# Channel MLP of a hybrid encoder: the down projection in pairs of hidden blocks with seven block products for eight, and the order of four engines written out

## The chip, the cores and the metric

One core of a Trainium2 chip runs the whole program in one launch. The metric is the device time of that core in microseconds. Engines are named as in the profile: PE is TensorE (matmuls; PEld its weight loads), DVE is VectorE, ACT is ScalarE, POOL is GpSimd, SP is SyncE, which here only issues DMAs.

## The reference

Two layers run over a prompt of 256 tokens and a sample of 1024 tokens with the same weights. Layer 0 mixes tokens with a bidirectional RWKV-7 recurrence, layer 1 with neighbourhood attention. Each layer ends with a squared-ReLU MLP; the change lies in that MLP and what surrounds it.

```python
D_MODEL = 1024; SEQ = 256; DEC_SEQ = 1024; D_FF = 4 * D_MODEL

def _sq_relu_mlp(h, w_up, w_down):
    return jnp.square(jax.nn.relu(h @ w_up)) @ w_down

def _trunk(x, p):
    for layer in range(DEPTH):
        h = _rms_norm(x, p['norm_mix_g'][layer])
        y = ...                                   # RWKV-7 (layer 0) or neighbourhood attention (layer 1)
        x = x + y
        x = x + _sq_relu_mlp(_rms_norm(x, p['norm_mlp_g'][layer]), p['w_up'][layer], p['w_down'][layer])
    return x
```

All data are fp32.

## The kernel before

Tokens of both requests stand side by side as 1280 columns in three segments: 0 is the prompt (256 columns), 1 and 2 are the halves of the sample (512 each). Channels lie on the 128 partitions, so 1024 channels are 8 tiles.

An fp32 product is made of three matmuls on rounded parts. Each operand is split into a high part (a cast to fp32r on ACT) and a low part (the operand minus its high part, on DVE or POOL); `mm3` adds high by high, high by low and low by high into one PSUM bank. `wsplit` (L80 to L91) loads a weight block (512 KB), casts it on ACT and subtracts on the engine it is given.

`channel_layer` (L1275 on) does the mixer's output projection, the residual, the norm and the MLP of one layer:

- the projection with `w_o` or `w_no`, eight output tiles, segments 0 and 1 together and then segment 2; its results are added to `x`, and `add_squares` gathers the sums for the norm;
- `scale(s)`: the normed input of the MLP isn't divided by its root mean square. Instead `x` is multiplied by the mean square `ms`, and the end of the MLP multiplies the sum by the reciprocal (`inverse`), which the homogeneous squared ReLU allows;
- the hidden dimension of 4096 goes in 32 blocks of 128. `up(f, s)` (L1353) makes block f for segment s: 24 matmuls over the 8 input tiles (`dense`), ReLU on ACT, square on POOL, high part on ACT, low part on DVE;
- `down(fs, s)` (L1371) multiplies the hidden blocks fs by their rows of `w_down`, into the 8 output tiles one after the other: three matmuls for each block and tile, then DVE adds the PSUM bank to `x` (L1382).

The loop of blocks runs `up(f, s)` and `down([f - 1], s)` for the three segments in turn. The last two blocks are summed in PSUM (`down([30, 31], s)`). In layer 0 each finished output tile is also scaled, stored, split for the next layer's projections (`split_x`) and squared (`add_squares`), and `token_norms` (N) and the first value blocks of the attention (`v_block`, V) are placed between output tiles.

The framework's planner sets the order of instructions on each engine, from its own estimates, except inside `manual_schedule`, where the engines named keep the order in which the program is written. Before, that holds for TensorE alone, from the last downs on. DMA issues on SP stay with the planner in both kernels. A tile of a pool has a name (tag) and `bufs` buffers in rotation; a writer waits until the last reader of the buffer's former content is done. PSUM has one ring of 7 banks (`ps`) and one bank for norms.

Of the kernel before, what the change touches and what calls it, by code (L numbers as in the profile page):

```python
# [13 lines left out]
P = 128  # L14
# [21 lines left out]

class Pieces:
# [11 lines left out]
class Trunk:  # L49
    def __init__(self, ctx, tc, a):  # L50
# [16 lines left out]
        self.dall = self.cp.tile([P, 8, 2, 20], F32, name="dall")  # L67
        self.bonus = self.cp.tile([P, 20, 8], F32, name="bonus")
# [436 lines left out]
    def v_block(self, act, vw, dst, tp, pp, q, tb, scale=1.0, later=False):  # L505

        nc = self.nc
        ps = pp[0].tile([P, 512], F32, name="vps", tag=pp[1])
# [648 lines left out]
    def add_squares(self, wk, x, m, s, acc, nsq=2):  # L1157

        nc = self.nc
        c0, c1 = SEGS[s]  # L1160
        n = c1 - c0
        if m == 0:
            nc.scalar.activation(acc[:, :n], x[s][:, m], AF.Square)
        else:
            sq = wk.tile([P, 512], F32, name="sq", tag="sq", bufs=nsq)
            nc.scalar.activation(sq[:, :n], x[s][:, m], AF.Square)
            nc.gpsimd.tensor_tensor(out=acc[:, :n], in0=acc[:, :n], in1=sq[:, :n], op=ALU.add)
# [9 lines left out]
    def token_norms(self, wk, wh_, pn, acc, s):  # L1177
# [8 lines left out]
        for j in range(2):  # L1186
            for b in range(nb):
                if j and b % 2 == 0:

                    w = 4 // nb  # L1190
                    pq = wh_.tile([P, 256], F32, name="pq", tag="hhFalse", bufs=2)
# [12 lines left out]
    def gate_begin(self):  # L1204
# [36 lines left out]
        def weight(m):  # L1241
            self.wo.append(self.wsplit(self.clw, self.a["w_o"][m], 1024, nc.gpsimd, tag="u"))
# [11 lines left out]
    def gated(self, wk, pm, src):  # L1254

        nc, act = self.nc, self.act
        with self.gctx, self.tc.tile_pool(name="go", bufs=1, reuse_waits="tile", side="right") as gp:
            (sh, sl, ss), (gh, gl, gs) = self.gate
            todo = [(0, k) for k in range(KT)] + [(s, k) for s in (1, 2) for k in range(KT - 1)] + [(1, KT - 1), (2, KT - 1)]
            for s, k in todo:  # L1260
# [5 lines left out]
                ps = pm.tile([P, 512], F32, name="ps", tag="ps")  # L1266
# [7 lines left out]
    def channel_layer(self, layer, x_src, src, wname, dst, gnext=None, gate=False):  # L1274
# [6 lines left out]
        with ExitStack() as ctx:  # L1281
# [7 lines left out]
            pn = ctx.enter_context(tc.tile_pool(name="cln", bufs=1, space=PSUM, reuse_waits="tile"))  # L1289
            wo = self.wo  # L1290
            if gate:
                self.gated(wk, pm, src)
# [13 lines left out]
            def dense(hi, lo, s):  # L1306
                c0, c1 = SEGS[s]
                n = c1 - c0
                ps = pm.tile([P, 512], F32, name="ps", tag="ps")
# [7 lines left out]
            for seg in ((0, 1), (2,)):  # L1317
                for m in range(8):
                    hi, lo = wo.pop(0)
                    if len(wo) < 1 and todo:  # L1320
                        wo.append(self.wsplit(wp, a[wname][todo.pop(0)], 1024, nc.vector, tag="u"))
# [9 lines left out]
                    for s in seg:  # L1331
# [3 lines left out]
                        self.add_squares(wk, x, m, s, ms[s], 2 + layer)  # L1335
# [17 lines left out]
            def up(f, s):  # L1353
                c0, c1 = SEGS[s]
                n = c1 - c0
                if s == 0:
                    wu[f] = self.wsplit(wp, a["w_up"][layer, f], 1024, nc.gpsimd, tag="u")
                ps = dense(*wu[f], s)
                r = wk.tile([P, 512], F32, name="rl", tag="nt", bufs=3 + layer)
                nc.scalar.activation(r[:, :n], ps[:, :n], AF.Relu)  # L1360
                nc.gpsimd.tensor_tensor(out=r[:, :n], in0=r[:, :n], in1=r[:, :n], op=ALU.mult)  # L1361
                hh, hl = (wh_.tile([P, c1 - c0], F32R, name=t, tag=f"{t}{s > 0}", bufs=4 if s else 2) for t in ("hh", "hl"))
                nc.scalar.copy(hh[:, :n], r[:, :n])  # L1363
                nc.vector.tensor_tensor(out=hl[:, :n], in0=r[:, :n], in1=hh[:, :n].bitcast(F32), op=ALU.subtract)  # L1364
                hid[f, s] = hh, hl

            def wdown(f):
                wd[f] = self.wsplit(wd_, a["w_down"][layer, f], 1024, nc.gpsimd, tag="d", rb=1)

            def down(fs, s, between={}):  # L1370
                c0, c1 = SEGS[s]  # L1371
                n = c1 - c0
                parts = [(wd[f], hid.pop((f, s))) for f in fs]
                last = NF - 1 in fs
                if last and gnext is not None:
                    accs[s] = wk.tile([P, 512], F32, name="acc", tag="acc", bufs=2) if s < 2 else wh_.tile([P, 512], F32, name="acc", tag="hhTrue", bufs=4)
                for m in range(8):
                    ps = pm.tile([P, 512], F32, name="ps", tag="ps")
                    for i, ((hi, lo), (hh, hl)) in enumerate(parts):
                        self.mm3(ps[:, :n], hi[:, m * P:(m + 1) * P], lo[:, m * P:(m + 1) * P], hh[:, :n], hl[:, :n], i == 0, i == len(parts) - 1)  # L1380
# [11 lines left out]
            wu, wd, hid, accs = {}, {}, {}, {}  # L1392
            rest = [(s, j) for s, (c0, c1) in enumerate(SEGS) for j in range((c1 - c0) // P)]
            up(0, 0)
            scale(0)
            wdown(0)
            up(1, 0)
# [3 lines left out]
            up(0, 2)  # L1401
            down([0], 0)
# [3 lines left out]
            down([0], 2)  # L1406
            wdown(1)
            for f in range(2, NF - 1):
                for s in range(3):
                    up(f, s)  # L1410
                    down([f - 1], s)
                if rest and f > 4:
                    inverse(*rest.pop())
                wdown(f)
            up(NF - 1, 0)
            up(NF - 1, 1)
            wdown(NF - 1)
            norms = lambda s: self.token_norms(wk, wh_, pn, accs[s], s)
            vw = []

            def block(tb):
                self.v_block(act, vw, self.scr["v1_d"], (wk, "nt", 512, 3), (pm, "ps"), 0, tb, self.tn[:, 0, tb:tb + 1])
            N = lambda s: lambda: norms(s)
            V = lambda tb: lambda: block(tb)
            with tc.manual_schedule(engines={mybir.EngineType.PE}):
                down([NF - 2, NF - 1], 0)
                up(NF - 1, 2)
# [493 lines left out]
```

## Time and profile before

| | |
|---|---|
| time, median of 3 runs | 4051.72 us (4046.44 to 4057.34) |
| span of the profiled execution (first to last instruction) | 4029.3 us; its own device time is not among the three, which lie 17 to 28 us above the span |
| PE busy | 3805.9 us, 94% of the span |
| DVE, ACT, POOL busy | 2244.2, 1580.9, 1338.7 us |
| MLP loop of layer 0, of layer 1 | from about 1545 to 2354 us, from about 3180 to 3992 us of the span |

How to read the lines below: a row of a time view gives start, duration, engine, source line, operation, output and input with their shapes, and in brackets how long the engine stood idle before it and for whom. A row of the windows view gives the stretch, its length, the busy times of PE, PEld, DVE, ACT and POOL (with counts), the granted clock of TensorE as a share of full speed, the DMA share and GB/s. Rows of groups give count, total and mean duration. Matmuls overlap in the records: their distance from start to start is the rate.

### The profile page before, as it was taken

How to read it: one execution, taken by the hardware profiler on the slowest of the kernel's cores; microseconds unless marked ns; L12 is line 12 of the kernel's file. 1: busy time of each engine (PE TensorE's matmuls, PEld its weight loads, DVE VectorE, ACT ScalarE, POOL GpSimd, SP SyncE). 2: the span in 40 equal slices, each digit the busy share in tenths (PEclk: the TensorE clock that was granted, in tenths of full speed). 3: DMA queues.
4: the chain of work that ended last, by engine and by line, in shares of the span. 5: the costliest groups of instructions: out<-in, count | busy, mean ns of one | idle time of the engine just before them, and what ended most of it. 6: DMA issues, size and time to landing. Idle time of an engine off the chain costs nothing.

```text
span 4029.3 us, 90997 instructions
## 1 busy us (share of the span) xinstructions
PE 3805.9 (94%) x36820; PEld 3210.5 (80%) x36820; DVE 2244.2 (56%) x4581; ACT 1580.9 (39%) x3868; POOL 1338.7 (33%) x1252
## 2 busy tenths in 40 slices
PE   8988898888888899999999999999989999999999
PEld 5764578778888788888888889887778888888888
DVE  5778743656564456555555561455554755555555
ACT  6776642555555431111111142565654111111111
POOL 4446542122222433222222250344443422222222
PEclk9987989999999999999999999999999999999999
DMA  4236565766664421101111015354463010110101
GB/s 140 72 104 221 207 222 137 171 171 160 161 153 118 146 79 37 42 32 42 37 37 43 32 71 165 103 124 98 101 199 129 35 42 35 39 42 32 42 32 63
DMA packets 450885, 394.89 MB, mean 98 GB/s; under 512 B 267456, under 2 KB 352832, under 8 KB 450464
## 3 DMA queue, kind: packets, MB, share of 16 engines
q1 hardware_dynamic: 416048, 327.72, 28.7%
q10 hardware_dynamic: 34416, 61.35, 4.1%
q8 instruction: 289, 4.73, 0.5%
q14 instruction: 132, 1.08, 0.1%
HBM read 270.50 MB, written 124.44 MB: 98 GB/s over the span
## 4 chain that ended last, share of the span: by engine, by line
PE 79%; DVE 6%; ACT 5%; DMA 4%; issue 4%; POOL 2%; SPq 1%; ACTq 0%; DVEq 0%; POOLq 0%
PE ps L95 19%; PE ps L96 19%; PE ps L97 19%; PE wu L997 4%; PE vps L512 1%; PE vps L513 1%; PE vps L514 1%; PE aps L997 1%; PE op L1836 1%; PE kps L997 1%; PE lps L997 1%; PE pt L1779 1%; PE ltw L598 1%; PE yps L997 1%; PE yo L997 1%
## 5 line engine op out<-in xcount | busy, mean ns | idle before, releaser
L1382 DVE TENSOR_TENSOR x<-ps,x 128x256 f32<-128x256 f32 x1488 | 814.5, 597 | 643.8 <-PE ps L97 643.7
L95 PE MATMUL ps<-ah,whi 128*128 128x512 f32 (+1 forms) x2304 | 843.2, 366 | 0.0
L96 PE MATMUL ps<-al,whi 128*128 128x512 f32 (+1 forms) x2304 | 825.5, 358 | 0.0
L97 PE MATMUL ps<-ah,wlo 128*128 128x512 f32 (+1 forms) x2304 | 822.6, 357 | 1.5 <-DVE wlo L90 1.3
L90 POOL TENSOR_TENSOR wlo<-raw,whi 128x1024 fp32r<-128x1024 f32 (+1 forms) x178 | 390.2, 2192 | 856.0 <-ACT whi L89 823.8
L95 PE MATMUL ps<-hh,whi 128*128 128x512 f32 (+1 forms) x1536 | 546.5, 356 | 9.8 <-DVE x L1382 9.8
L96 PE MATMUL ps<-hl,whi 128*128 128x512 f32 (+1 forms) x1536 | 545.6, 355 | 0.0
L97 PE MATMUL ps<-hh,wlo 128*128 128x512 f32 (+1 forms) x1536 | 545.1, 355 | 0.0
L95 PEld LDWEIGHTS ps<-ah,whi 128*128 128x128 f32 x2304 | 434.3, 188 | 72.4 <-issue 8.2
L97 PEld LDWEIGHTS ps<-ah,wlo 128*128 128x128 f32 x2304 | 433.4, 188 | 72.6 <-DVE wlo L90 1.7
L96 PEld LDWEIGHTS ps<-al,whi 128*128 128x128 f32 x2304 | 434.4, 189 | 62.3 <-issue 1.0
L89 ACT CAST whi<-raw 128x1024 fp32r<-128x1024 f32 (+1 forms) x206 | 200.4, 973 | 706.3 <-PE ps L96 627.7
L1361 POOL TENSOR_TENSOR rl<-rl 128x512 f32<-128x512 f32 (+1 forms) x192 | 173.8, 905 | 506.1 <-PE ps L97 462.4
L95 PEld LDWEIGHTS ps<-hh,whi 128*128 128x128 f32 x1536 | 290.7, 189 | 54.2 <-DVE x L1382 12.0
L97 PEld LDWEIGHTS ps<-hh,wlo 128*128 128x128 f32 x1536 | 291.0, 189 | 41.6
L96 PEld LDWEIGHTS ps<-hl,whi 128*128 128x128 f32 x1536 | 290.6, 189 | 40.5
L1360 ACT ACTIVATE rl<-ps 128x512 f32<-128x512 f32 (+1 forms) x192 | 100.7, 524 | 555.9 <-PE ps L97 555.9
L1363 ACT CAST hh<-rl 128x512 fp32r<-128x512 f32 (+1 forms) x192 | 105.6, 550 | 324.2 <-POOL rl L1361 324.2
L1364 DVE TENSOR_TENSOR hl<-rl,hh 128x512 fp32r<-128x512 f32 (+1 forms) x192 | 119.8, 624 | 143.1 <-ACT hh L1363 142.5
L1773 POOL TENSOR_TENSOR s<-s,mx 128x384 f32<-128x384 f32 (+1 forms) x150 | 109.7, 744 | 163.2 <-DVE mx L1772 114.2
L872 DVE TENSOR_TENSOR tmp<-mt,q 128x31 f32<-128x31 f32 (+15 forms) x310 | 117.2, 378 | 38.9 <-ACT mt L861 21.0
L1078 POOL TENSOR_TENSOR y<-y,mu 128x512 f32<-128x512 f32 x18 | 19.3, 1074 | 351.2 <-DVE mu L1075 351.2
(304 smaller groups left out, 8265.1 us busy)
## 6 DMA issues: line engine op xcount, KB each, us to landing
raw<-in_w_down_dram SPq DMA_DIRECT2D x64, 512.0 KB
raw<-in_w_up_dram SPq DMA_DIRECT2D x64, 512.0 KB
ar<-ar_d SPq DMA_DIRECT2D x80, 256.0 KB
bk<-bk_d SPq DMA_DIRECT2D x80, 256.0 KB
ar_d<-ar ACTq DMA_DIRECT2D x32, 512.0 KB
bk_d<-bk ACTq DMA_DIRECT2D x32, 512.0 KB
bs<-tab SPq DMA_DIRECT2D x128, 96.0 KB
v_d<-vt ACTq DMA_DIRECT2D x80, 128.0 KB
```

What stands on the lines that cost most here:

```text
L89: nc.scalar.copy(hi[:, cs], raw)
L90: lo_eng.tensor_tensor(out=lo[:, cs], in0=raw, in1=hi[:, cs].bitcast(F32), op=ALU.subtract)
L95: mm(ps, sh, mh, start=first, stop=False)
L96: mm(ps, sh, ml, start=False, stop=False)
L97: mm(ps, sl, mh, start=False, stop=last)
L872: nc.vector.tensor_tensor(out=tv, in0=mt[:, 0:jj, jj:jj + 1].to_broadcast([P, jj, w]), in1=q[:, jj:jj + 1, jj:].to_broadcast([P, jj, w]), ...
L997: self.nc.tensor.matmul(out, w, x, start=start, stop=stop, skip_group_check=free)
L1361: nc.gpsimd.tensor_tensor(out=r[:, :n], in0=r[:, :n], in1=r[:, :n], op=ALU.mult)
L1363: nc.scalar.copy(hh[:, :n], r[:, :n])
L1364: nc.vector.tensor_tensor(out=hl[:, :n], in0=r[:, :n], in1=hh[:, :n].bitcast(F32), op=ALU.subtract)
L1382: nc.vector.tensor_tensor(out=xv, in0=ps[:, :n], in1=xv, op=ALU.add)
L1773: nc.gpsimd.tensor_tensor(out=s[:, :nk], in0=s[:, :nk], in1=mx[:, 2:3].to_broadcast([P, nk]), op=ALU.mult)
```

## The change

For the sample (segments 1 and 2) two hidden blocks and two halves of the output channels form a 2 x 2 by 2 x 2 block product: weights A(i, j) of 128 rows x 512 output channels, with i the half of the output and j the block of the pair, times hidden parts b(j, t), with t the segment. It is done with seven products of sums instead of eight plain ones, in the form with shared partial sums: `pair_steps` defines for each step n a `prep(n)` (the weight sum on POOL and its split into W[n]; the hidden sum on DVE and its split into B[n]), a `product(n)` (4 output tiles, three matmuls of 512 columns each; where the shared sum goes on, the matmuls add to the bank that DVE has just read) and a `prompt(n)`, which uses four of the split weights for the prompt's plain products, two output tiles in one bank. `block_pair` writes out the order: the next pair's ups between the products of the current one. There are 14 such pairs (blocks 2 to 29) in each layer; blocks 0, 1, 30 and 31 go as before.

From block 2's up to the end of `channel_layer`, TensorE, DVE, ACT and POOL all keep the written order. Further: `w_down` is loaded in halves of 256 KB with six raw buffers; the other weights of the layer have one raw buffer where they had two; the seven PSUM banks become rings of 3 (`ps`) and 4 (`pc`); `inverse` is called once per pair; the constants `dall` and `bonus` live in a pool that closes before the first `channel_layer`.

```diff
+MANUAL = {mybir.EngineType.PE, mybir.EngineType.DVE, mybir.EngineType.Activation, mybir.EngineType.Pool}
...
+            def bank(name=None):
+                turn[0] += 1
+                name = name or ("ps", "pc")[turn[0] % 2]
+                return pm.tile([P, 512], F32, name="ps", tag=name, bufs={"ps": 3, "pc": 4}[name])
...
+            def wup(f):
+                wu[f] = self.wsplit(wp, a["w_up"][layer, f], 1024, nc.gpsimd, tag="u", rb=1)
+
+            def split(src, s, pool, tags, bufs, eng):
+                n = src.shape[1]
+                hi, lo = (pool.tile([P, n], F32R, name=t, tag=t, bufs=bufs) for t in tags)
+                nc.scalar.copy(hi, src)
+                eng.tensor_tensor(out=lo, in0=src, in1=hi.bitcast(F32), op=ALU.subtract)
+                return hi, lo
...
+            def up(f, s, name=None, whole=True):
...
+                ps = dense(*wu[f], s, name)
+                r = wk.tile([P, n], F32, name="rl", tag="nt", bufs=6) if s else wh_.tile([P, n], F32, name="rl", tag="np", bufs=2)
+                nc.scalar.activation(r, ps[:, :n], AF.Relu)
+                nc.gpsimd.tensor_tensor(out=r, in0=r, in1=r, op=ALU.mult)
+                hid[f, s] = r
+                if whole or s == 0:
+                    cut(f, s)
+
+            def wraw(f, i):
+                r = raws[f, i] = wd_.tile([P, 512], F32, name="raw", tag="dr", bufs=6)
+                nc.sync.dma_start(r, a["w_down"][layer, f, :, 512 * i:512 * i + 512])
+
+            def wcut(src):
+                return split(src, 0, wd_, ("dh", "dl"), 4, nc.gpsimd)
...
+            def pair_steps(f0, f1):
+                W, B, S, ch = {}, {}, {}, {}
+                A = lambda i, j: raws[(f0, f1)[j], i]
+                b = lambda j, t: hid[(f0, f1)[j], t]
+                tt = lambda eng, o, x_, y_, op: eng.tensor_tensor(out=o, in0=x_, in1=y_, op=op)
+                bcut = lambda src: split(src, 1, wh_, ("hhTrue", "hlTrue"), 3, nc.vector)
...
+                def prep(n):
+                    if n == 0:
+                        W[0], B[0] = wcut(A(0, 1)), bcut(b(1, 1))
+                    elif n == 1:
+                        S["s"] = stile()
+                        tt(nc.gpsimd, S["s"], A(1, 0), A(1, 1), add)
+                        S["t"] = ttile()
+                        tt(nc.vector, S["t"], b(0, 2), b(0, 1), sub)
+                        W[1], B[1] = wcut(S["s"]), bcut(S["t"])
+                    elif n == 2:
+                        tt(nc.gpsimd, S["s"], S["s"], A(0, 0), sub)
+                        s4 = stile()
+                        tt(nc.gpsimd, s4, A(0, 1), S["s"], sub)
+                        W[2], B[2] = wcut(s4), bcut(b(1, 2))
+                    elif n == 3:
+                        W[3], B[3] = wcut(A(0, 0)), bcut(b(0, 1))
...
+                    elif n == 5:
+                        s3 = stile()
+                        tt(nc.gpsimd, s3, A(0, 0), A(1, 0), sub)
+                        t3 = ttile()
+                        tt(nc.vector, t3, b(1, 2), b(0, 2), sub)
+                        W[5], B[5] = wcut(s3), bcut(t3)
...
+                    elif n == 7:
+                        W[7] = wcut(A(1, 0))
+
+                def product(n):
+                    new, seg, row = ((1, 1, 0), (1, 2, 4), (0, 2, 0), (1, 1, 0), (0, 2, 0), (0, 2, 4), (0, 1, 4))[n]
+                    (hi, lo), (hh, hl) = W[n], B[n]
+                    for j in range(4):
+                        if new:
+                            ch[j] = bank("pc")
+                        cs = slice(j * P, j * P + P)
+                        mm = nc.tensor.matmul
+                        mm(ch[j], hi[:, cs], hh, start=bool(new), stop=False, skip_group_check=True)
+                        mm(ch[j], hi[:, cs], hl, start=False, stop=False, skip_group_check=True)
+                        mm(ch[j], lo[:, cs], hh, start=False, stop=True, skip_group_check=True)
+                        xv = x[seg][:, row + j]
+                        nc.vector.tensor_tensor(out=xv, in0=ch[j], in1=xv, op=ALU.add)
...
+            def block_pair(f2, cur, ahead):
+                (prep, product, prompt), f3, final = cur, f2 + 1, ahead is None
+                U = lambda f, s: up(f, s, "ps", False)
+                prep(1)
+                product(0)
+                prompt(0)
+                U(f2, 1)
+                wraw(f3, 0)
+                prep(2)
+                product(1)
+                U(f2, 2)
+                wraw(f2, 1)
+                prep(3)
+                product(2)
+                U(f2, 0)
+                if not final:
+                    wup(f2 + 2)
+                prep(4)
+                product(3)
+                prompt(3)
+                U(f3, 1)
+                wraw(f3, 1)
+                prep(5)
+                product(4)
+                if not final:
+                    U(f3, 2)
+                prep(6)
+                product(5)
+                prep(7)
+                U(f3, 0)
+                wraw(f2, 0)
+                if not final:
+                    wup(f3 + 2)
+                product(6)
+                prompt(6)
+                if not final:
+                    ahead[0](0)
+                prompt(7)
...
-            for f in range(2, NF - 1):
-                for s in range(3):
-                    up(f, s)
-                    down([f - 1], s)
-                if rest and f > 4:
-                    inverse(*rest.pop())
-                wdown(f)
...
+            with tc.manual_schedule(engines=MANUAL):
...
+                for f in range(2, NF - 2, 2):
+                    ahead = pair_steps(f + 2, f + 3) if f < NF - 4 else None
+                    block_pair(f + 2, cur, ahead)
+                    cur = ahead
+                    if rest and f > 4:
+                        inverse(*rest.pop())
...
+                up(NF - 1, 2, None, False)
+                cut(NF - 1, 2, True)
                 down([NF - 2, NF - 1], 0)
-                up(NF - 1, 2)
...
+                    v0 = [self.wsplit(wp, ..., 1024, nc.gpsimd, tag="u", rb=1) for j in range(2)]
```

136 lines of the change are left out of this document (90 added, 46 removed).

## The prediction

> **What bounds the kernel now.** I read the page's chain first, then the busy time by stretches of both MLP loops, then the instructions in order of time of one pass of the loop and of the end of layer 0's MLP.
>
> ```profile
> span 4029.3 us, 90997 instructions
> PE 79%; DVE 6%; ACT 5%; DMA 4%; issue 4%; POOL 2%; SPq 1%; ACTq 0%; DVEq 0%; POOLq 0%
> ```
> ```profile
> 2200.00:2300.00 100.00, 100.00 (x529) 85.81 (x528) 53.03 (x99) 19.69 (x30) 28.82 (x19) 1.00 0.12 43
> 3530.91:3558.83 27.92, 27.92 (x145) 23.76 (x144) 14.71 (x27) 5.23 (x9) 7.46 (x5) 1.00 0.11 38
> 2375.00:2396.00 21.00, 15.87 (x94) 13.07 (x92) 20.52 (x29) 8.87 (x17) 14.18 (x9) 0.99 0.25 94
> ```
> The chain is 79% TensorE. In the two loops TensorE is busy in every microsecond at full granted clock (PEclk, the column behind the five busy times), and one pass over a hidden block takes 27.92 us in which DVE works 14.71, ACT 5.23 and POOL 7.46 us. Only removed matmuls shorten a pass. The third row is the end of layer 0's MLP: there DVE is busy 20.52 of 21 us and TensorE waits.
>
> **The change, part by part**
>
> *Matmuls removed.* First matmuls of the four groups of one pass (start, duration):
> ```profile
> 3508.51 0.28 PE L95 MATMUL ps<-ah,whi 128*128 128x256 f32 x1
> 3511.38 0.28 PE L95 MATMUL ps<-hh,whi 128*128 128x256 f32 x1
> 3514.25 0.39 PE L95 MATMUL ps<-ah,whi 128*128 128x512 f32 x1
> 3519.85 0.40 PE L95 MATMUL ps<-hh,whi 128*128 128x512 f32 x1
> 3525.34 0.39 PE L95 MATMUL ps<-ah,whi 128*128 128x512 f32 x1
> ```
> From start to start: up on the prompt 2.87, down on the prompt 2.87, up on one half of the sample 5.60, down on it 5.49 us. A pair of blocks had eight half-products of 5.49 / 2 = 2.745 us each on the sample; now it has seven. 14 pairs in 2 layers: 28 x 2.745 = **-76.9 us**, if TensorE stays full. A pair then lasts 2 x 27.92 - 2.745 = 53.1 us.
>
> *Work added beside it.* Means by shape:
> ```profile
> L1382 DVE TENSOR_TENSOR x<-ps,x 128x512 f32<-128x512 f32 x992 | 637.3, 686 | 601.2 <-PE ps L97 601.1
> L90 POOL TENSOR_TENSOR wlo<-raw,whi 128x1024 fp32r<-128x1024 f32 x142 | 343.8, 2421 | 763.7 <-ACT whi L89 763.7
> L90 POOL TENSOR_TENSOR wlo<-raw,whi 128x512 fp32r<-128x512 f32 x36 | 46.4, 1288 | 92.3 <-ACT whi L89 60.1 <-DMA vraw<-in_w_nv_dram 24.5 <-PE ps L97 3.8
> L1361 POOL TENSOR_TENSOR rl<-rl 128x512 f32<-128x512 f32 x128 | 133.2, 1041 | 504.6 <-PE ps L97 462.4 <-ACT rl L1360 42.1
> L1364 DVE TENSOR_TENSOR hl<-rl,hh 128x512 fp32r<-128x512 f32 x128 | 90.8, 709 | 115.2 <-ACT hh L1363 114.8
> L1363 ACT CAST hh<-rl 128x512 fp32r<-128x512 f32 x128 | 79.6, 622 | 269.3 <-POOL rl L1361 269.3
> L1360 ACT ACTIVATE rl<-ps 128x512 f32<-128x512 f32 x128 | 76.1, 595 | 434.5 <-PE ps L97 434.5
> L89 ACT CAST whi<-raw 128x1024 fp32r<-128x1024 f32 x170 | 178.2, 1048 | 637.4 <-PE ps L96 622.5 <-issue 5.9 <-DMA raw<-in_w_down_dram 5.7
> ```
> Per pair POOL gets eight half-weight subtractions (8 x 1.29), two whole ones (2 x 2.42), the squares (4 x 1.04 + 2 x 0.6) and four weight sums (priced like a subtraction, 4 x 1.29): 26 us against 14.9. DVE gets 36 evictions of 512 columns (28 for products, 8 for the prompt's two-chunk banks, where there were 32 plus 16 short ones), seven low parts (7 x 0.71), four sums, two short low parts and about one reciprocal: 34 us against 29.4. ACT: about 15 against 10.4. All lie below 53, so no engine takes over as an average. The half-size weight loads double 64 DMA issues on SP, whose queue is idle in between; the bytes stay. The cost is then in the order, since DVE, ACT and POOL now run strictly as written.
>
> *The hand-over between pairs.* I walked through one pair with these durations. Nearly all operands are ready over 1 us ahead, because a block of up (5.6 us) lies behind each preparation. The exception is step 0 of the next pair, written between the last two prompt groups. How a short up passes through the engines:
> ```profile
> 3511.58 0.39 ACT L1360 ACTIVATE rl<-ps 128x256 f32<-128x256 f32 x1 [2.06 <-PE ps L97]
> 3512.04 0.61 POOL L1361 TENSOR_TENSOR rl<-rl 128x256 f32<-128x256 f32 x1
> 3512.68 0.41 ACT L1363 CAST hh<-rl 128x256 fp32r<-128x256 f32 x1 [0.72 <-POOL rl L1361]
> 3513.12 0.43 DVE L1364 TENSOR_TENSOR hl<-rl,hh 128x256 fp32r<-128x256 f32 x1 [0.40 <-ACT hh L1363]
> 3969.78 3.67 DVE L1382 TENSOR_TENSOR x<-ps,x 128x512 f32<-128x512 f32 x6
> ```
> With X the end of the last short up (3511.38 here), its low part is done at X+2.17. ACT then casts the new up weight (to X+2.7), POOL subtracts it (X+2.74 to X+5.14) and only then the weight of step 0 (to X+6.40). DVE meanwhile evicts four product chunks and two prompt banks back to back (0.61 apart, last row) and reaches the low part of step 0 at X+5.7. Whether it can run there:
> ```profile
> 2384.10 1.41 POOL L1167 TENSOR_TENSOR acc<-acc,sq 128x512 f32<-128x512 f32 x1 [0.27 <-ACT sq L1166]
> 2384.30 0.68 DVE L1382 TENSOR_TENSOR x<-ps,x 128x512 f32<-128x512 f32 x1
> 2384.91 1.16 DVE L1175 SCALAR_TENSOR_TENSOR al<-x,vec,ah 128x512 fp32r<-128x512 f32 x1
> 2372.98 1.29 POOL L1384 TENSOR_TENSOR x<-x,ms 128x512 f32<-128x512 f32 x1
> 2373.71 1.11 DVE L1364 TENSOR_TENSOR hl<-rl,hh 128x512 fp32r<-128x512 f32 x1 [4.21 <-ACT hh L1363]
> ```
> An eviction (one input in PSUM) ran its normal 0.68 beside a POOL subtraction or sum, but operations with two SBUF inputs ended 0.56 and 0.55 us after POOL's (2385.51 to 2386.07; 2374.27 to 2374.82). So the low part ends at X+6.40+0.55 = X+6.95. TensorE wants it for the second matmul of product 0: product 6 (2.745) and two prompt groups (1.435 each) and one matmul, X+5.85. Stall 1.15 us. Without the exclusion DVE would end at X+6.4, a stall of 0.6; were that operand early, the low part of the weight (X+6.40, wanted by the third matmul at X+6.1) would be late next, by 0.3. 13 hand-overs x 2 layers x 1.15 = **+30 us** (16 without the exclusion; at the low end 0, if DVE reaches the operand earlier than walked).
>
> The Trainium skill, "SBUF — State Buffer", section "Who interferes with whom", says that a VectorE instruction with two SBUF inputs and a GpSimd instruction that reads SBUF exclude each other for the whole instruction. The trace agrees with its 0.55 us behind POOL's end. By that rule the hand-overs cost the 30 us just taken and the sum below is 4042; with free sharing they would cost 16, and it would be 4028.
>
> *The last pair* of a layer has no up between products 4 and 5, and product 5 adds onto banks that DVE must first read. The low part of step 5 stands ahead of these evictions on DVE and comes some 5.5 us after the start of product 4 (relu 0.6, square 1.04, weight sum 1.29, cast 0.62, subtraction 1.29, 0.55 of exclusion); the first eviction ends at 6.2 where TensorE asks at 2.745. **+3.5 per layer, +7**.
>
> *The end of layer 0's MLP*, so far ordered by hand on TensorE alone, is now in written order on all four. Rows of before:
> ```profile
> 2355.17 0.42 DVE L1382 TENSOR_TENSOR x<-ps,x 128x256 f32<-128x256 f32 x1 [4.34 <-PE ps L97]
> 2367.49 0.68 DVE L1382 TENSOR_TENSOR x<-ps,x 128x512 f32<-128x512 f32 x1
> 2412.81 4.14 DVE L1175 SCALAR_TENSOR_TENSOR al<-x,vec,ah 128x512 fp32r<-128x512 f32 x3
> 2437.66 0.48 ACT L518 ACTIVATE vt<-vps,tn 128x256 f32<-128x256 f32 x1 [1.52 <-PE vps L514]
> 2374.74 0.74 DVE L1175 SCALAR_TENSOR_TENSOR al<-x,vec,ah 128x512 fp32r<-128x512 f32 x1
> 2378.47 0.72 ACT L1174 ACTIVATE ah<-x,vec 128x512 fp32r<-128x512 f32 x1 [2.52 <-DVE x L1384]
> ```
> The first row is the first eviction; the prompt's splits last 12.3 us, the sample's 49.5 (2367.49 to 2416.95), the value blocks end 20.7 later: 82.5 us, with the last up hidden inside. Written order makes each output chunk a loop through engines: eviction 0.6, scaling, ACT's high part 0.75, DVE's low part 0.77, and only then the next eviction; POOL's sum of squares of the chunk before (1.3) holds the port. A chunk scaled on DVE takes 0.6 + wait to 1.3 + 0.55 + 0.75 + 0.77 = 3.4; one scaled on POOL 1.3 + 1.3 + 0.75 + 0.77 = 4.1; eight chunks 28.7 (the first POOL one lacks the sum: 3.5). Two halves: 57.4, and two chains of norms between them (an estimate of 2 each, some ten steps of 0.15 to 0.4): 62. The prompt at 0.42/0.69 of that: 17. The second value weight has one raw buffer now, so its load follows the first one's subtraction, and ACT waits in front of the sample's first chunk:
> ```profile
> 3506.55 0.33 SPq L88 DMA_DIRECT2D raw<-in_w_up_dram  x1
> 3507.50:3509.50 2.00, 2.00 (x15) 1.79 (x14) 1.29 (x3) 1.65 (x2) 0.02 (x1) 1.00 0.78 258
> ```
> A 512 KB load takes about 3 us from issue to the end of its traffic; with cast and subtraction it delays the chain by 7.5. The last hidden block's cut (up, square, cast, subtraction) stands ahead of the first eviction, +2.6, and its up (5.6) now precedes the chain. 5.6 + 2.6 + 17 + 7.5 + 62 + 20.7 = 115.4 against 82.5: **+33 us** (+15 if the chunks overlap better, +45 with a cold clock). Layer 1's end has no such loop: nothing.
>
> *The start of the MLP.* Ten reciprocals per layer ran there (the last two rows are layer 1's):
> ```profile
> L90 DVE TENSOR_TENSOR wlo<-raw,whi 128x1024 fp32r<-128x1024 f32 x28 | 34.6, 1235 | 5.0 <-ACT whi L89 5.0
> 3149.90 2.58 DVE L1351 RECIPROCAL ms<-ms 128x128 f32<-128x128 f32 x3
> 3152.80 0.39 PE L95 MATMUL ps<-hh,whi 128*128 128x256 f32 x1 [3.15 <-DVE x L1382]
> ```
> Three of them stand just ahead of the evictions for which TensorE waits 3.15 us. They move into the pairs, where DVE has 19 us of slack: -3 per layer. Single raw buffers for the projection and up weights make a chain of load 3.05, cast 1.05 and subtraction 1.24 per output chunk, beside 5.6 us of matmuls: it just fits; I put +1.5 per layer for the second up weight. Together **-3** (-6 to +6). The moved constants and the two PSUM rings (7 banks as before) I put at nothing: their last readers end before the first writers here.
>
> Sum: -76.9 + 30 + 7 + 33 - 3 = -10, on the profiled span of 4029.3: 4019. The median of the runs is 22.4 above that span; what lies around the span I leave as it is: 4051.7 - 10 = **4042 us**. The bounds: pairs 0 to 84 (below), end 15 to 45, start -6 to +6.
>
> **The rivals**
>
> *Faster: the pairs run full.* If DVE reaches step 0 without the backlog I walked, the 30 us go: 4012. For it: DVE has 19 us of slack per pair. Against it: the whole weight's subtraction (2.42) stands ahead of step 0 on POOL.
>
> *Faster: the end of layer 0 overlaps as before.* With +10 instead of +33: 4019. For it: before, DVE was full there too (20.52 of 21), so part of my loop may replace waits that already exist. Against it: written order leaves DVE idle during ACT's part of each chunk.
>
> *Slower: up weights land late.* If SP issues the second up weight in written order, it goes behind the last half weight of the next pair, whose buffer frees with POOL's subtraction for step 7, at about X-0.6 (the last sample up ends at X-5.6; relu 0.6, square 1.04, two subtractions of 1.29, one exclusion of 0.55). 768 KB at the rate of the row above (258 GB/s) end near X+3.7, ACT casts there instead of X+1.6, and step 0 slips by 2.1: the stall becomes 3.25, 26 x 3.25 = 84 instead of 30: 4096. It decides once the weight lands after X+2.45 (0.85 us x 26 = 22 more brings it to 4064). Against it: in the trace SP issues the up weight as soon as its buffer is free (3506.55, half a pass ahead of need).
>
> **How the numbers follow.** About 0.3%, 12 us, is what a measurement of this kernel can tell from no change. My forecast has 0.45, with its own range of 4022 to 4062 (0.14 faster, 0.27 same, 0.04 slower); full pairs 0.25 (faster); a better end 0.13 (faster, 0.03 of it same); late weights 0.15 (slower); the rest 0.02. Faster 0.49, same 0.32, slower 0.19. The range of 8 in 10 runs from 4005 to 4082: below it lie full pairs together with a better end, above it the full price of late weights.
>
> **What would show it.** The matmuls of the two loops drop by 336. Between pairs TensorE waits about 1.1 us for a DVE low part, 26 times, at a period near 54.3 us; without these waits full pairs are right, with 3 us late weights. Behind product 4 of the last pair stands one wait of 3 to 4 us for evictions. From the first eviction of layer 0's last down to its last value block there are 105 to 115 us, with DVE waiting for ACT's high parts. The waits of 3.2 us at the MLP's start shrink below 1. Wrong would be the whole picture if POOL or DVE were busy nine tenths of a pair.

## The result and the profile after

The changed kernel takes 4076.97 us in the median of 4 runs (4066.76 to 4086.64), the kernel before 4049.09 (4 runs): ratio 1.0066, 95% interval 1.0045 to 1.0087. It is slower, by 18 to 35 us; 10 us less were forecast. A second series further down gave 1.0070 [1.0055, 1.0085].

The page of the profile after: span, chain, and the groups in which TensorE waits (behind the bar busy time, mean of one, and the idle time ahead with what ended most of it).

```profile
span 4084.8 us, 89789 instructions
PE 69%; DVE 10%; DMA 7%; ACT 6%; issue 4%; POOL 3%; SPq 1%; ACTq 0%; POOLq 0%; DVEq 0%
L96 PE MATMUL ps<-ah,whi 128*128 128x512 f32 (+1 forms) x2304 | 846.1, 367 | 7.9 <-ACT whi L90 7.1
L98 PE MATMUL ps<-ah,wlo 128*128 128x512 f32 (+1 forms) x2304 | 828.3, 360 | 6.2 <-POOL wlo L91 5.3
L1477 PE MATMUL ps<-hlTrue,dh 128*128 128x512 f32 x784 | 311.5, 397 | 15.1 <-DVE hlTrue L1368 15.1
L1476 PE MATMUL ps<-hhTrue,dh 128*128 128x512 f32 x784 | 308.5, 394 | 7.2 <-DVE x L1480 7.2
```
TensorE's share of the chain fell from 79% to 69%, DVE's rose from 6% to 10%. Two of the waits are new in kind: the first two groups, up and projection, had none on a weight worth telling before and now stand 7.1 us for casts on ACT and 5.3 us for low parts on POOL. In e4 below, with two half buffers, they are 2.4 us and none; in e9, the kernel before with single buffers alone, 3.2 and 6.5.

The stages, cut at TensorE's first matmul of each; an MLP start runs from its first norm matmul to the last matmul of block 1's downs, a loop from there to the last downs or the last up ahead of them, so that this up counts to the end in both (us; in brackets an unedited second run of the changed kernel, a0 below):

| stage | before | after | difference |
|---|---|---|---|
| up to layer 0's projection | 1377.5 | 1405.5 (1393.7) | +28.0 (+16.2) |
| of it, end of the scan: last zk cut to last root | 21.0 | 28.1 (26.5) | +7.1 (+5.5) |
| layer 0's projection | 115.3 | 114.4 (113.9) | -0.9 (-1.4) |
| MLP start, layer 0 | 74.4 | 82.4 (79.7) | +8.0 (+5.3) |
| loop, layer 0 | 787.3 | 777.3 (776.2) | -10.0 (-11.1) |
| end of layer 0's MLP | 91.8 | 124.9 (124.9) | +33.1 (+33.1) |
| attention | 562.0 | 567.9 (564.9) | +5.9 (+2.9) |
| layer 1's projection | 117.4 | 120.0 (118.8) | +2.6 (+1.4) |
| MLP start, layer 1 | 75.5 | 82.6 (81.2) | +7.1 (+5.7) |
| loop and end, layer 1 | 828.1 | 809.7 (811.3) | -18.4 (-16.8) |

The spans differ by 55.5, twice what the medians do: the profiled execution of before was faster than all its timed runs, that of after was the slowest of its four. Most of the 28 us ahead of the projection seems of that kind (the same kernel reached it at 1405.5 and at 1393.7); about 6 of them belong to the change (below).

The steady pair, the last pair's products 4 and 5, and the first wait of layer 0's end, from the windows of after:

```profile
1670.63:1725.09 54.46, 53.72 (x279) 45.35 (x277) 33.25 (x50) 14.06 (x25) 27.37 (x21) 1.00 0.13 39
2358.62:2361.38 2.76, 2.76 (x13) 2.06 (x11) 0.00 (x0) 0.60 (x1) 1.83 (x2) 1.00 0.00 0
2361.38:2365.10 3.72, 0.15 (x1) 0.02 (x1) 2.08 (x3) 1.66 (x3) 2.99 (x3) 0.89 0.21 70
2365.10:2370.37 5.27, 5.26 (x13) 4.11 (x14) 4.59 (x8) 1.14 (x2) 1.67 (x2) 0.50 0.01 3
2406.50:2437.60 31.10, 0.57 (x6) 0.44 (x4) 13.70 (x17) 9.93 (x16) 14.91 (x11) 0.59 0.21 76
```
A pair takes 54.46 us with DVE busy 33.3, POOL 27.4 and ACT 14.1 (forecast 54.3, 34, 26 and 15): none of the three is near full. Product 4 of the last pair runs its 2.76 us, then TensorE stands 3.72; the fourth row is taken up in the last section. At the end of layer 0 TensorE works 0.57 us out of 31.1.

The hand-over between two pairs, rows of after in order of time:

```profile
1664.60 0.40 PE L1476 MATMUL ps<-hhTrue,dh 128*128 128x512 f32 x1
1666.35 0.42 DVE L1368 TENSOR_TENSOR hlFalse<-rl,hhFalse 128x256 fp32r<-128x256 f32 x1 [2.44 <-ACT hhFalse L1367]
1667.34 2.41 POOL L91 TENSOR_TENSOR wlo<-raw,whi 128x1024 fp32r<-128x1024 f32 x1 [1.47 <-ACT whi L90]
1669.70 1.30 POOL L1368 TENSOR_TENSOR dl<-raw,dh 128x512 fp32r<-128x512 f32 x1
1670.28 1.27 DVE L1368 TENSOR_TENSOR hlTrue<-rl,hhTrue 128x512 fp32r<-128x512 f32 x1
1670.63 0.39 PE L1476 MATMUL ps<-hhTrue,dh 128*128 128x512 f32 x1
1671.60 0.50 PE L1477 MATMUL ps<-hlTrue,dh 128*128 128x512 f32 x1 [0.58 <-DVE hlTrue L1368]
```
Product 6 starts here at X = 1664.60. The short up's low part ends at X+2.17, the up weight's subtraction at X+5.15, step 0's weight at X+6.40, and DVE's low part of step 0, begun beside it, at X+6.95, 0.55 behind POOL's end: within 0.01 us, the figures of the walk in the prediction. Only TensorE came otherwise. The last two prompt groups took 3.29 us where 2.87 were walked, because they waited for a PSUM bank that DVE had not yet read, so product 0 (last two rows) starts at X+6.03 and not at X+5.62. Its second matmul starts at X+7.00, 1.15 us behind the X+5.85 of the walk.

### The profile page after: what moved, and what is told of

It is laid out like the page before. It is cut to its first block, busy times and chain, and to the rows that moved or that the text cites. A ratio compares the mean times of both kernels' runs of the same rounds, so it can differ in the third digit from the quotient of the medians.

```text
span 4084.8 us, 89789 instructions
## 1 busy us (share of the span) xinstructions
PE 3778.3 (92%) x36484; PEld 3171.2 (78%) x36484; DVE 2337.9 (57%) x4441; ACT 1686.3 (41%) x4128; POOL 1688.6 (41%) x1540
## 4 chain that ended last, share of the span: by engine, by line
PE 69%; DVE 10%; DMA 7%; ACT 6%; issue 4%; POOL 3%; SPq 1%; ACTq 0%; POOLq 0%; DVEq 0%
PE ps L96 12%; PE ps L98 12%; PE ps L97 12%; PE ps L1477 4%; PE wu L998 4%; PE ps L1476 4%; PE ps L1478 4%; DVE x L1480 2%; PE vps L513 1%; PE vps L514 1%; PE vps L515 1%; PE aps L998 1%; PE kps L998 1%; PE op L2001 1%; PE lps L998 1%
## 5 line engine op out<-in xcount | busy, mean ns | idle before, releaser
L1480 DVE TENSOR_TENSOR x<-ps,x 128x512 f32<-128x512 f32 x784 | 484.9, 678 | 0.1
L91 POOL TENSOR_TENSOR wlo<-raw,whi 128x1024 fp32r<-128x1024 f32 (+1 forms) x114 | 235.2, 2064 | 223.0 <-ACT whi L90 211.6
L1477 PE MATMUL ps<-hlTrue,dh 128*128 128x512 f32 x784 | 311.5, 397 | 15.1 <-DVE hlTrue L1368 15.1
L1476 PE MATMUL ps<-hhTrue,dh 128*128 128x512 f32 x784 | 308.5, 394 | 7.2 <-DVE x L1480 7.2
L1478 PE MATMUL ps<-hhTrue,dl 128*128 128x512 f32 x784 | 308.1, 393 | 0.5 <-POOL dl L1368 0.5
L1368 DVE TENSOR_TENSOR hlTrue<-ts,hhTrue 128x512 fp32r<-128x512 f32 x112 | 139.3, 1244 | 217.7 <-ACT hhTrue L1367 217.7
L90 ACT CAST whi<-raw 128x1024 fp32r<-128x1024 f32 (+1 forms) x142 | 133.1, 937 | 189.2 <-PE ps L97 71.4
L1368 POOL TENSOR_TENSOR dl<-raw,dh 128x512 fp32r<-128x512 f32 x128 | 196.5, 1546 | 12.4 <-ACT dh L1367 11.0
L1368 POOL TENSOR_TENSOR dl<-ds,dh 128x512 fp32r<-128x512 f32 x112 | 169.0, 1509 | 63.4 <-ACT dh L1367 63.4
L1477 PEld LDWEIGHTS ps<-hlTrue,dh 128*128 128x128 f32 x784 | 147.8, 188 | 52.1 <-DVE hlTrue L1368 23.4
L1476 PEld LDWEIGHTS ps<-hhTrue,dh 128*128 128x128 f32 x784 | 147.9, 189 | 38.6 <-issue 8.0
```

Of the source, the lines that this page charges most:

```text
L90: nc.scalar.copy(hi[:, cs], raw)
L91: lo_eng.tensor_tensor(out=lo[:, cs], in0=raw, in1=hi[:, cs].bitcast(F32), op=ALU.subtract)
L1368: eng.tensor_tensor(out=lo, in0=src, in1=hi.bitcast(F32), op=ALU.subtract)
L1476: mm(ch[j], hi[:, cs], hh, start=bool(new), stop=False, skip_group_check=True)
L1477: mm(ch[j], hi[:, cs], hl, start=False, stop=False, skip_group_check=True)
L1478: mm(ch[j], lo[:, cs], hh, start=False, stop=True, skip_group_check=True)
```

## The experiments

Times are compared by their ratio to the kernel before, timed beside each; the changed kernel itself has 1.0066 to 1.0070, so 0.001 is 4 us.

**The end of layer 0: written order on TensorE alone (e1_tail).**
```diff
                 cut(NF - 1, 2, True)
+            with tc.manual_schedule(engines={mybir.EngineType.PE}):
                 down([NF - 2, NF - 1], 0)
```


> Only layer 0's (and layer 1's) end is edited: from the last two downs on, only TensorE keeps the written order, as in the kernel before. Theory W (the written order of DVE, ACT and POOL makes the first norms wait behind later evictions): the stretch from the last up group of layer 0 (31, second half of the sample) to the end of its last V block falls from 116 us to 83 to 86, the 31 us wait of TensorE ahead of the first norms' transposes falls below 3, and the time falls by 30 to 33 us, to 4044 to 4047. Rival R1 (the buffers of the new layout set the end: rings shared by relu outputs, squares and V tiles, single raw buffer of the V weights): the stretch stays above 110 us and the time within 5 us of 4077. In both, all other stages stay.

Ratio 1.0011 [0.9993, 1.0030]. The stretch from the end of the last up to the attention's first matmul went from 119.6 to 90.9 us, -28.7: theory W. Counted as in the expectation, from the start of the last up to the last V block, it went from 116.3 to 87.3, a little above 83 to 86; by the ratios the time fell by 22 to 24 us where 30 to 33 were expected. What ACT did in that stretch of after:

```profile
2405.00 1.04 ACT L90 CAST whi<-raw 128x1024 fp32r<-128x1024 f32 x1
2412.58 1.04 ACT L90 CAST whi<-raw 128x1024 fp32r<-128x1024 f32 x1 [6.54 <-DMA raw<-in_w_nv_dram]
2418.57 0.72 ACT L1175 ACTIVATE ah<-x,vec 128x512 fp32r<-128x512 f32 x1 [3.80 <-POOL x L1418]
2436.05 0.72 ACT L1175 ACTIVATE ah<-x,vec 128x512 fp32r<-128x512 f32 x1 [1.99 <-DVE x L1418]
2437.20 0.39 ACT L1193 COPY pq<-acc 128x256 f32<-128x256 f32 x1
PE nps L1196 <- ACT pq L1193: 36.8, 2, 30.6
```
TensorE waits 30.6 us for a copy of 0.39 us (`pq`, last two rows). The prompt's norms are written behind output tile 6 of the next down, so the copy stands in ACT's order behind the second value weight's cast (6.54 us for its load) and six passes of one cast each (2418.57 to 2436.05, two passes per 7.1 us), each waiting for the next scaled tile. In e1 TensorE's waits in this stretch add up to 13 us: 6.4 for evictions and 5.7 for the sums that the norms need are the largest.

**The rest of the end (e8_cover).** The kernel of e1 with the last up behind the first of the last downs again:
```diff
-                up(NF - 1, 2, None, False)
-                cut(NF - 1, 2, True)
...
                 down([NF - 2, NF - 1], 0)
+                up(NF - 1, 2, None, False)
+                cut(NF - 1, 2, True)
```


> The kernel with only TensorE in written order at the end of a layer, with the last up group again between the first and the second of the last downs, as in the kernel before. Theory C (the end of layer 0 is as long as DVE's evictions, cuts and norms; the last up group covers 5.6 us of them only when it lies behind the first down): from the end of the products to the attention 95 us in place of 99.7, some 4.6 less than that kernel, ratio to the kernel before about 1.0000. Rival R8 (the 4.6 come from the shared rings): the same 99 to 100.

Ratio 0.9990 [0.9976, 1.0003]; from the end of the products to the attention 94.5 in place of 99.7 us:
```profile
2375.30:2475.00 99.70, 86.87 (x546) 78.89 (x545) 70.51 (x112) 43.44 (x93) 51.47 (x39) 0.91 0.33 107
2365.40:2459.90 94.50, 83.98 (x546) 77.08 (x545) 69.86 (x111) 42.66 (x92) 50.03 (x39) 0.95 0.35 112
```
The first row is e1, the second e8. DVE has 70 us of work in both; the last up covers 5 of them only behind the first down (theory C).

**The hand-over: step 0 cut early (e2_early).**
```diff
                 prep(7)
+                if not final:
+                    ahead[0](0)
                 U(f3, 0)
...
                 prompt(6)
-                if not final:
-                    ahead[0](0)
                 prompt(7)
```


> Only the place of the next pair's step 0 changes: its two operand cuts are written right behind step 7's, ahead of the short up and the up weight's cut, and no longer between the last two prompt groups. Theory H (product 0 waits for its operand because it is cut last, behind the up weight on POOL and six evictions on DVE): product 0 goes from 3.60 to 2.75 us, the last prompt group from 3.29 per two to 2.87, the pair from 54.4 to 53.1 us; 26 hand-overs x 1.27 = 33 us less, 4044. If the bank wait of the last prompt group stays, 26 x 0.85 = 22 less, 4055. Rival R2 (DVE has no room in this place: the early cut only pushes evictions back, and another product waits): the pair stays at 54.1 or more, the time within 5 us of 4077.

Ratio 1.0034 [1.0020, 1.0048]: 13 to 15 us less, under half of the 33. Waits of TensorE in layer 0's pairs (total, times, longest), after and then e2:

```profile
PE ps L1477 <- DVE hlTrue L1368: 7.6, 13, 0.6
PE ps L96 <- DVE x L1491: 2.1, 13, 0.2
PE ps L96 <- DVE x L1491: 6.7, 13, 0.5
```
The wait for step 0 is gone, that for a free bank grew. From start to start, product 0 went from 3.61 to 2.75 us, the last two prompt groups from 3.29 to 3.64, the pair from 54.46 to 53.95. Neither theory had this: the stall of 0.86 went, and the one ahead of the prompt groups' banks grew by 0.35, from 0.42 to 0.77.

**The short up's cut behind product 6 (e6_cut), on top of e2.** The new last argument of `up` leaves the cut out.
```diff
-                U(f3, 0)
+                up(f3, 0, "ps", False, True)
...
                 product(6)
+                cut(f3, 0)
```


> The kernel with step 0 cut early, and besides the cast and low part of the last short up are written behind product 6 in place of ahead of it. Theory D (with step 0 early, DVE stood in order at the short up's low part, some 2.2 us behind the up's end, and product 6's evictions and so the banks of the last prompt groups came late: 0.78 us in place of 0.42): both stalls go, the pair falls from 53.95 to 53.2 us, 26 x 0.75 = 20 us less than with step 0 early alone, 4040. Rival R5 (three banks are too few for four prompt banks in a row, whatever DVE does): the pair stays at 53.9 and the time at 4059.

Ratio 1.0002 [0.9985, 1.0018]. The prompt groups take 3.01 us, the pair 53.32 in layer 0 and 53.18 in layer 1: theory D. DVE had stood in written order at the short low part with product 6's first eviction (due at X+0.7) queued behind. Rows of e2, where X is 1653.69:

```profile
1655.80 0.43 DVE L1368 TENSOR_TENSOR hlFalse<-rl,hhFalse 128x256 fp32r<-128x256 f32 x1 [2.20 <-ACT hhFalse L1367]
1656.14 2.48 DVE L1480 TENSOR_TENSOR x<-ps,x 128x512 f32<-128x512 f32 x4
```
The first eviction comes at X+2.45.

**The last up of the sample inside the last pair (e3_lastu).**
```diff
                 product(4)
-                if not final:
-                    U(f3, 2)
+                U(f3, 2)
...
-                up(NF - 1, 2, None, False)
```


> Only the last pair of each layer changes: the last up group of the sample stands between products 4 and 5, as in the other pairs, and not behind the pair. Theory L (with no up between them DVE's cut of step 5 lies ahead of product 4's evictions): products 4 and 5 take 5.5 us without the up in place of 11.75 in layer 0 and 9.34 in layer 1, so about 10 us less, 4067. Rival R3 (the weight of step 5, cut on POOL, is as late): a wait of 2 us or more is left there in each layer, less than 6 us gained.

Ratio 1.0042 [1.0026, 1.0057]. Products 4 and 5 take 2.77 us each in layer 0 and 2.73 in layer 1: theory L.

**The raw buffers (e4_half, and e9_raw1 on the kernel before).** e4 has two raw buffers of half the size for all 1024-column weights (`rb=1` becomes `cuts=2`, with `rb` at 2):

> Only the raw buffers of the 1024-column weights change: two of half the size (loaded, cast and subtracted by halves) in place of one. Theory B (with a single raw buffer a load starts only when the weight before has been subtracted, so weights come late where they follow closely): layer 1's projection goes from 120.0 to 115 us, the MLP starts from 83.2 and 82.7 to 78 to 79, together 12 to 15 us less, 4062 to 4065. Rival R4 (the MLP starts are longer by the written order and PSUM rings): starts and projection stay, or get longer by the added instruction overheads, time 4077 to 4085.

e9 is the kernel before with `rb=1` at the same four places:

> The kernel before, with one raw buffer in place of two for the 1024-column weights (gate, projections, up, V) and nothing else. Theory B (the single buffer alone costs the changed kernel about 25 us): scan's end 5 to 6 us longer, layer 1's projection 2 to 3, each MLP start 7 to 10, together 21 to 29 us, ratio 1.005 to 1.007. Rival R9 (the starts got longer by the written order and the halved down weights): 5 to 9 us, from the gate and the projection alone.

e4: ratio 0.9986 [0.9971, 1.0001], the largest gain of one edit. The time fell by some 32 us where theory B expected 12 to 15. The two MLP starts take 71.6 and 71.4; in the eight profiles with the written order and the single buffer they take 79.5 to 82.6. The stall at product 0 fell from 0.86 to 0.57, which no theory had. Layer 1's projection stayed at 119.9, so theory B fails there. The halves change two things, the number of buffers and the size of a piece; e9 changes the number alone. e9: ratio 1.0049 [1.0029, 1.0068], 20 us, just under theory B's range and far from rival R9. Its MLP starts take 81.7 and 82.0 against 75.5 and 75.4 in e5 below, its scan's end 27.4 against 21.3, together 18.9; its layer 1's projection stayed at 117.4. Waits of TensorE at layer 0's MLP start, two rows of after, one of e4, two of e9 and, last, one of before:

```profile
PE ps L98 <- POOL wlo L91: 3.4, 2, 2.4
PE ps L96 <- ACT whi L90: 0.8, 2, 0.6
PE ps L96 <- DVE x L1416: 1.7, 3, 0.9
PE ps L97 <- POOL wlo L90: 3.2, 2, 1.9
PE ps L95 <- ACT whi L89: 1.2, 2, 0.6
PE ps L95 <- DVE x L1382: 4.4, 3, 3.2
```
The waits for weights come with the single buffer and go with two halves; no written order is in e9.

**The gate (e7_gate).**
```diff
-        at(11.4, weight, 1)
+        at(13.0, weight, 1)
```


> The changed kernel, with the second weight of layer 0's projection asked for later in the scan's plan (13.0 in place of 11.4). Theory G (with one raw buffer the second weight's load waits for the first one's subtraction on POOL, and its cast, next in ScalarE's order, stands some 4 us ahead of the copies that the scan's last chunks wait for): the stretch from the last zk cut to the last reciprocal root of the scan goes from 26 to 28 us back to 21, the time from 1.0068 of the kernel before to about 1.0054, 5 to 6 us. Rival R7 (the stretch is longer by the gate's other changes): it stays at 26 or more.

Ratio 1.0055 [1.0035, 1.0075]; the stretch is 20.3 us. The time moved by 5 us, as expected, but within its interval; the stretch decides. The two casts of the projection's first weights on ACT, in before, in after and in e7:

```profile
1329.72 1.04 ACT L89 CAST whi<-raw 128x1024 fp32r<-128x1024 f32 x1
1332.40 1.05 ACT L89 CAST whi<-raw 128x1024 fp32r<-128x1024 f32 x1
1350.60 1.04 ACT L90 CAST whi<-raw 128x1024 fp32r<-128x1024 f32 x1
1357.58 1.04 ACT L90 CAST whi<-raw 128x1024 fp32r<-128x1024 f32 x1 [4.19 <-DMA raw<-in_w_o_dram]
1341.16 1.04 ACT L90 CAST whi<-raw 128x1024 fp32r<-128x1024 f32 x1
1348.41 1.05 ACT L90 CAST whi<-raw 128x1024 fp32r<-128x1024 f32 x1
```
In after the second cast waits 4.19 us for a load that could not start before the first weight's subtraction (that ends at 1354.08, the load is issued at 1354.11), and the scan's copies wait behind it on ACT. In e7 it comes 7.25 us after the first too, but other work stands in between.

**The moved constants (e5_lead) and the changed kernel again (a0).** e5 is the kernel before with `dall` and `bonus` in a pool of their own, as in the change.

> The kernel before, with one part of the change: the two small tiles of the first layer live in a pool of their own that closes ahead of the MLP. Theory V (the 28 us by which the changed kernel's profile reached layer 0's projection later are variation between executions, not the change): time within 6 us of 4047, and the profile reaches the projection between 1385 and 1410 us, as any execution. Rival R6 (the moved tiles cost in the first stages, by other addresses or waits of the pool): 4060 or more.

> The changed kernel once more, unedited, beside the others: 4070 to 4080 in the median; its profile reaches layer 0's projection between 1390 and 1410 us (by theory V it moves by more than 5 us against 1405.5; by R6 it doesn't), and every stage behind it has the lengths of the first profile within 3 us, the attention within 6.

e5: ratio 1.0003 [0.9990, 1.0017]; its profile reached the projection at 1380.1 us, earlier than theory V's 1385. The pool costs nothing. a0: 4066.44 us, below the range written for its median, and ratio 1.0070. It reached the projection at 1393.7. The other kernels' profiles lie between 1385.3 and 1407.8. So the place varies by over 10 us between executions; but both profiles with two full raw buffers are the earliest, by 3 us up to the scan's last zk cut (1331.0 and 1332.2, all others 1334.9 to 1355.5). Whether a few of those microseconds belong to the change stays open, and so does the length of the attention (562.0 and 565.3 in the two, 564.5 to 573.3 in the others).

**All edits together (b3, b4).** b3 joins e1, e2, e6, e3 and e4. b4 adds e7 and moves `cut(f3, 0)` behind `prompt(6)`.

> All edits together: end of the layer with TensorE alone in written order, step 0 cut early, short up cut behind product 6, last up between products 4 and 5, raw up weights in two halves. By the stages of the single edits: starts 21 us less, the two ends and the last pairs 29 and 10 less, hand-overs 26 x 1.27 = 33 less, together 93 less than 4077: 3984, which is 63 under the kernel before. If the edits share a cause (the halves already took 8 us of the hand-overs), 8 us more, 3992. Rival: written order without slack loses again elsewhere (DVE or POOL now ahead of TensorE by less than 1 us): over 4000.

> All edits together and two more: the second gate weight asked for later, and the short up's cut behind prompt group 6 in place of ahead of it. With theory G 5 us less at the scan's end; the two last prompt groups go from 3.15 and 3.19 to 2.87 and 2.84 us, 26 x 0.3 = 8 less: ratio to the kernel before from 0.9858 to 0.9825 to 0.983. If DVE's order has no room there, product 0's prompt group waits for the short operand and the 8 us stay.

b3: 3982.53 us, against 4039.91 of the kernel before in its series: ratio 0.9858 [0.9841, 0.9875], 57 us less. That lies between the 63 of edits that simply add up and the 55 of the variant in which the halves had already taken 8 us of the hand-overs; its pair takes 53.46 us in layer 0, not the 53.2 of no stall. b4: 3981.47 us against 4051.07, ratio 0.9838 [0.9820, 0.9857], 1.6% under the kernel before. Two passes of before in layer 0 and one pair of b4, also in layer 0:
```profile
1573.13:1628.73 55.60, 55.60 (x290) 47.47 (x289) 29.34 (x55) 10.46 (x16) 14.93 (x10) 1.00 0.11 39
1641.52:1694.69 53.17, 53.17 (x278) 45.25 (x277) 32.09 (x51) 14.21 (x28) 27.97 (x22) 1.00 0.13 40
```
TensorE is busy in all of 53.17 us. A pair of b4 is shorter than two passes of before by 2.4 us in layer 0 (53.18 against 55.60) and by 2.85 in layer 1 (52.99 against 55.84), over 28 pairs 74 of the 77 us of the forecast's first term: the seven products give nearly all of it once the order costs nothing; whether b4 is faster than b3, the intervals leave open.

## Why the prediction was wrong

The step that failed is the start of the MLP with its price of single raw buffers, fifth in this list: forecast -3, measured +13, and +6 more at the scan's end.

- *Matmuls removed, -76.9*: right. 336 matmuls of 512 columns are gone, and b4 loses nothing of it but about 3 us: in layer 0 four of the seven products take 2.77 us, half a down of before 5.45 / 2.
- *Hand-overs, +30*: right in mechanism and nearly in size. Product 0 takes 0.86 longer and the last two prompt groups 0.42: 1.28 x 26 = 33. The walk had left out the bank. It cost little here, because product 0 would have waited those 0.42 us for its operand anyway; it showed only when step 0 came early (e2).
- *Last pair, +7*: the wait is 3.6 to 3.7 where 3.5 was said. In layer 0 it had a consequence that was left out (2.5 us, last section): 10 in all.
- *End of layer 0, +33*: right, +33.1, with the wait for the second value weight (7.5 said) at 6.54 on ACT and 7.7 on DVE. That the written order of DVE, ACT and POOL makes it is shown by e1.
- *Start of the MLP, -3*: this step failed, in its term "+1.5 per layer" for the single raw buffers: the starts came out at +13 in place of -3. By e9 the single buffer costs 6 to 7 per layer, against e4's halves 8 to 11; what lies between the two is open. It costs 6 more at the scan's end, where the diff's `rb=1` in the gate was priced at nothing. The term compared a chain of load 3.05, cast 1.05 and subtraction 1.24 with 5.6 us of matmuls. That is the chain of a projection weight, which DVE subtracts, and there it fits (layer 1's projection in e9). An up weight is subtracted on POOL, in 2.4 us, which makes 6.5; the first two of layer 0 in after are cast 7.14 apart:

```profile
1520.02 1.03 ACT L90 CAST whi<-raw 128x1024 fp32r<-128x1024 f32 x1
1521.12 2.37 POOL L91 TENSOR_TENSOR wlo<-raw,whi 128x1024 fp32r<-128x1024 f32 x1 [3.25 <-ACT whi L90]
1527.16 1.05 ACT L90 CAST whi<-raw 128x1024 fp32r<-128x1024 f32 x1 [0.28 <-DMA raw<-in_w_up_dram]
1529.71 2.33 POOL L91 TENSOR_TENSOR wlo<-raw,whi 128x1024 fp32r<-128x1024 f32 x1
```

TensorE waits there for both, the longest 2.4 us for the second subtraction. In the gate the waiting cast blocked a queue with other stages' work. The other term, -3 per layer for the reciprocals, fits: e4's starts lie 2.8 and 4.1 below before's, and TensorE's wait for evictions fell from 4.4 to 1.7 us; no run moves the reciprocals alone.

- *Moved constants and two rings at nothing*: the constants, yes (e5); the rings show in the hand-over's 0.42, and once step 0 came early they cost more (e2).

Measured terms: -76.9 + 33 + 10 + 33 + 13 (the starts, mean of both profiles) + 6 + 2 (layer 1's projection, whose cause no run shows) + 3 = +23, inside the 18 to 35 of the ratio. The attention (+3 to +6) and the rest of the way to layer 0's projection are left open. The starts and the gate alone, 19 in place of -3, turn the forecast of -10 into +12.

Of the rivals, the late up weights (4096) did not happen between the pairs: the second matmul of product 0 waited for DVE's low part 0.58, not for weights. Full pairs and a better end, the two faster ones, exist, but only in other orders (b4, e1). The measured 4077 lies inside the range of 4005 to 4082, by luck: the upper end stood there for the late up weights, and no rival had a dearer start. Slower had a chance of only 0.19: the bounds of -6 to +6 for the start could not turn a sum of -10, and the measured +13, with 6 at the scan's end, did. The 22.4 us between span and median, which the prediction laid to what lies around the span, were a fast profiled execution: in every run with both on record the time is 1.8 us above the span. The difference forecast does not hang on it.

## What to carry to other kernels

Price a buffer taken away at every place that uses the helper, with the engine that works there, not at one steady place: follow what is queued behind the instruction that will wait for it, also in the stages before. An order written out for four engines cost nothing in a loop whose engines have slack, once two cuts stood elsewhere (b4); whether the planner's own order would have done as well there, no run shows. Where a short copy releases another engine (the norms), leaving the order to the planner gave 28.7 us (e1); writing the copy ahead of the passes was not tried. If a stall of a written order goes away, look at what stood in order behind the moved instruction: here 0.77 of the 1.28 us stayed, at a bank, until a second instruction was moved.

## What the runs showed of the hardware

A wait can cost TensorE more than its length. In the windows above, 3.72 us without work are followed by 5.27 us at a granted clock of 0.50: product 5 takes 5.25 us in place of 2.75. In layer 1 the same place waited as long and the clock stayed:

```profile
2365.11 0.76 PE L1476 MATMUL ps<-hhTrue,dh 128*128 128x512 f32 x1 [3.58 <-DVE x L1480]
4035.05 0.47 PE L1476 MATMUL ps<-hhTrue,dh 128*128 128x512 f32 x1 [3.62 <-DVE x L1480]
4028.60:4038.00 9.40, 5.78 (x26) 4.49 (x25) 4.35 (x7) 2.92 (x6) 5.23 (x4) 1.00 0.09 30
```
Waits of 3.58 and 3.62 us stand in the brackets; behind the second the clock is 1.00 and product 5 took 2.83. The Trainium skill, "TensorE: Matmul & The Clock Gate", section "HAM oscillation — how this bites in real kernels", says to leave no gaps in TensorE's work above about 3.4 us, because the gate then goes back to half clock. The trace agrees with the half (0.50) and with the size of the gap, but shows that a gap a little above need not do it. What decides between the two, these runs do not show.
